# A hybrid decoder block with 64 experts on one core: other load sizes and room order in the expert pass, paired products in the gate pieces, idle products before the last transposes

## The chip, the cores and the metric

The kernel runs on one core of one Trainium2 chip. The metric is device time in microseconds (us) of one launch. Before the change, three runs took 1255.89, 1257.45 and 1258.70 us (median 1257.45). One more execution was profiled; it took 1255.22 us.

## The reference

All tensors are float32. 16 meta tokens are put ahead of 256 tokens of width 1024, so 272 rows go through the block.

```
hn   = rms_norm(h, norm_mix)
u, z, xbc, dt, g_pool, g_ssd = split(hn @ w_in)          # w_in: 1024 x 8224
y_pool = pool_mixer(u) @ w_pool_out                      # causal window means of 2, 4, 8, 16 rows
y_ssd  = ssd_mixer(z, xbc, dt) @ w_ssd_out               # Mamba-2 scan, 32 heads, chunks of 128
h = h + (sigmoid(g_pool) * y_pool + sigmoid(g_ssd) * y_ssd) @ w_out
x2 = rms_norm(h, norm_ffn)
# one expert group of 8 per token, then 2 of its 8 experts
y = sum over the token's 2 experts e: weight * (silu(x2 @ w_gate[e]) * (x2 @ w_up[e])) @ w_down[e]
out = rms_norm(h + y, norm_final)[16:]
```

The 64 experts' weights are 403 MB: w_gate_up is 64 x 1024 x 1024 and w_down 64 x 512 x 1024. All of them are read, whatever the routing.

## The kernel before

**Front.** `w_in` and the smaller weights come as 98 pieces of 128 x 1024, two to a load of 1 MB ("chunk", `load_w`, L194), into a ring of four chunks. The order of the work is written by hand: step n computes piece n (`proj`, L448, for the first 64) and then runs what was put down for that step (`at(n, ...)`, `hooks`). Float32 products are made of three products of split operands: `mm3` multiplies high by high, high by low and low by high. `split_piece` (L270) makes the high and the low half of a piece three pieces ahead: ScalarE (ACT) copies the high half, VectorE (DVE) or, for some pieces, GpSimd (POOL) subtracts it to get the low one. The second half of a chunk, once split, triggers the load of the chunk four further on. The 16 gate pieces ("gp" and "gs", steps 48 to 63) each end in one ACT Sigmoid read from PSUM. Then come the pooling products ("pw", L705 to L708), whose activations `pool_s(w)` splits on DVE into tiles "ah" and "al" of a pool of six buffers each (`asplit_f`); the splits for w = 0 to 2 are put down for steps 56, 58 and 60, the one for w = 3 stands inside the pooling stage, behind its first products. After them come "po" (8 pieces), "so" (16) and "wo" (8), then the router.

**Experts.** Experts are taken four at a time: 16 quads. A quad's weights are 24 rooms of 1 MB (128 partitions x 2048 floats): 16 of gate/up, read in `up(q, xT)`, and 8 of down, read in `down(q)`. Room m is number m mod 24 of quad m // 24. `load_e` (L207) issues the loads on SyncE's queue (SP), in order. The first 24 rooms are single loads into 24 places that come free one by one while the front still runs (arena, "aux", "ws", "mg"). From room 24 on, loads are of two rooms (2 MB, 16 KB per partition), into 11 places: eight in the arena, issued as the first pass gives them up (`freed`, L184: after rooms 1, 4, 6, 7, 9, 13, 16, 19), and three "pair" tiles, issued after room 23. From there on every odd room, once used (`used`, L227), issues the next load into the place it leaves. The last eight rooms are single loads again. At most eight loads are under way: each waits for the landing of the one eight before.

**One quad on TensorE (PE).** `up`: 128 matmuls of 32 x 512 per operand half, four per room; then two transposes (L958), the gather of the next quad's tokens (L933), `glu` (ACT Silu, DVE product, four transposes at L952, ACT copy), `down`: two halves of four rooms, each followed by an ACT copy and `combine` (L971), which adds into four PSUM accumulators. In the last quad `keep_warm` puts idle products (ones by ones) between rooms of `down` (`WARM`, L23: three each behind rooms (0,2), (0,3), (1,0), (1,1), (1,2), as half and room).

## Time and profile before

| what | value |
|---|---|
| runs, median | 1257.45 us (1255.89 to 1258.70) |
| the profiled execution | 1255.22 us, its span 1253.5 us |
| PE busy | 959.0 us, 77% of the span |
| DVE, ACT, POOL busy | 319.4, 291.2, 141.5 us |
| moved | 462.06 MB, mean 369 GB/s |

The span is what the page and all rows count from; the 1.7 us around it are launch and end. Engines overlap, so busy shares do not add up to the span: what matters is which wait ends last at each place. PE holds two sorts of row: PE for matmuls, PEld for loading the stationary operand, which runs beside them. A matmul's duration includes the time in which it overlaps its neighbours, so the pace of a run of matmuls is read from the distance of their starts. In rows of a time line the number in square brackets is the engine's idle time before the row, and what ended it.

### The profile page before, as it was taken

To read this page: it belongs to the slowest core of one execution; us is meant where nothing else is said; L and a number is where in the kernel's file an instruction comes from. 1 tells how busy PE (TensorE), PEld (TensorE's weight loads), DVE (VectorE), ACT (ScalarE), POOL (GpSimd) and SP (SyncE) were. 2 spreads that over 40 slices of the span, in tenths; PEclk is the share of its full clock that TensorE was granted. 3 is DMA by queue.
4 is the path that set the end of the run, shared out by engine and by line. 5 is a ranking of instruction groups with operands and counts; after the bars stand their busy time and mean duration, and the time that the engine had idled before them with its cause. 6 is when DMAs were issued, how large, how long until landed. Compare 5 with 4: busy or idle time off the path is not lost.

```text
span 1253.5 us, 15661 instructions
## 1 busy us (share of the span) xinstructions
PE 959.0 (77%) x6721; PEld 538.0 (43%) x6721; DVE 319.4 (25%) x529; ACT 291.2 (23%) x558; POOL 141.5 (11%) x118
## 2 busy tenths in 40 slices
PE   9999999999997767576775757575658666666766
PEld 9999999999853321212221212131222212121312
DVE  6899986668731000000000000000000000000001
ACT  7887756433331100101010101010100101010102
POOL 2334444334100000000000000000000000000000
PEclk9999999999999898888888888888988797888788
DMA  7544447667899999999999999999999999999996
GB/s 290 185 157 165 168 140 268 266 216 258 344 407 430 430 430 432 430 431 430 431 430 431 429 431 429 431 430 431 430 431 429 432 430 432 429 431 430 432 427 264
DMA packets 39656, 462.06 MB, mean 369 GB/s; under 512 B 4424, under 2 KB 4752, under 8 KB 6816
## 3 DMA queue, kind: packets, MB, share of 16 engines
q1 hardware_dynamic: 39216, 459.95, 88.3%
q8 instruction: 54, 0.88, 0.3%
q10 hardware_dynamic: 368, 1.08, 0.2%
q14 instruction: 18, 0.15, 0.0%
HBM read 459.93 MB, written 1.08 MB: 368 GB/s over the span
## 4 chain that ended last, share of the span: by engine, by line
DMA 62%; PE 26%; DVE 7%; ACT 3%; issue 1%; SPq 0%; POOL 0%; DVEq 0%; ACTq 0%; POOLq 0%
DMA arena<-gu 28%; DMA pair<-gu 15%; DMA arena<-dn 12%; DMA pair<-dn 6%; PE pj L297 3%; PE pj L299 3%; PE pj L298 3%; DVE whl L280 3%; PE pg L1045 1%; PE pg L1056 1%; PE pu L1045 1%; PE pj L769 1%; PE gx L933 1%; DVE arena L462 1%; PE so L298 1%
## 5 line engine op out<-in xcount | busy, mean ns | idle before, releaser
L1045 PE MATMUL pg<-arena,xT 128*32 128x512 f32 x776 | 121.8, 703 | 125.4 <-DMA arena<-gu 125.4
L959 DVE COPY aux<-tr 128x256 f32<-128x256 f32 x16 | 6.8, 425 | 682.6 <-PE tr L958 682.6
L924 ACT ACTIVATE xT<-gx,csta 128x128 f32<-128x128 f32 x124 | 35.4, 368 | 530.5 <-PE gx L933 522.8
L297 PE MATMUL pj<-hnh,whl 128*128 128x256 f32 (+1 forms) x512 | 149.7, 292 | 0.0
L299 PE MATMUL pj<-hnh,whl 128*128 128x256 f32 (+1 forms) x512 | 145.9, 285 | 0.4 <-DVE whl L280 0.4
L298 PE MATMUL pj<-hnl,whl 128*128 128x256 f32 (+1 forms) x512 | 145.7, 285 | 0.1
L1045 PE MATMUL pu<-arena,xT 128*32 128x512 f32 x768 | 125.1, 729 | 0.0
L280 DVE TENSOR_TENSOR whl<-arena,whl 128x1024 fp32r<-128x1024 f32 x79 | 115.2, 1465 | 30.4 <-ACT whl L279 29.9
L1045 PEld LDWEIGHTS pg<-arena,xT 128*32 128x32 f32 x776 | 18.6, 114 | 220.6 <-DMA arena<-gu 185.2
L975 POOL TENSOR_TENSOR aux<-sel,wte 128x128 f32<-128x128 f32 x32 | 12.2, 401 | 829.9 <-DVE sel L876 786.4
L279 ACT ACTIVATE whl<-arena 128x1024 fp32r<-128x1024 f32 x86 | 90.5, 1056 | 54.2 <-PE so L299 29.5
L297 PEld LDWEIGHTS pj<-hnh,whl 128*128 128x128 f32 x512 | 96.5, 189 | 2.5 <-issue 2.0
L298 PEld LDWEIGHTS pj<-hnl,whl 128*128 128x128 f32 x512 | 96.4, 188 | 1.2 <-issue 1.2
L299 PEld LDWEIGHTS pj<-hnh,whl 128*128 128x128 f32 x512 | 96.5, 189 | 0.6 <-DVE whl L280 0.6
L933 PE MATMUL gx<-sel,xh 128*128 128x128 f32 x480 | 65.0, 291 | 29.3 <-ACT xT L924 18.6
L971 PE MATMUL acc<-aux 128*128 128x512 f32 x128 | 63.5, 618 | 24.0 <-ACT aux L969 23.2
L1045 PE MATMUL pg<-pair,xT 128*32 128x512 f32 x240 | 41.4, 769 | 50.7 <-DMA pair<-gu 50.6
L933 PEld LDWEIGHTS gx<-sel,xh 128*128 128x128 f32 x480 | 59.1, 201 | 36.9 <-ACT xT L924 21.7
L1045 PEld LDWEIGHTS pu<-arena,xT 128*32 128x32 f32 x768 | 28.7, 127 | 72.5 <-issue 72.5
L1056 PE MATMUL pg<-arena,aux 128*32 128x512 f32 x328 | 53.9, 806 | 6.9 <-ACT aux L953 6.9
L280 POOL TENSOR_TENSOR whl<-arena,whl 128x1024 fp32r<-128x1024 f32 x19 | 47.8, 2521 | 74.1 <-ACT whl L279 73.7
L971 PEld LDWEIGHTS acc<-aux 128*128 128x128 f32 x128 | 21.7, 189 | 67.9 <-ACT aux L969 50.8
(343 smaller groups left out, 1208.6 us busy)
## 6 DMA issues: line engine op xcount, KB each, us to landing
arena<-gu SPq DMA_DIRECT2D x90, 2048.0 KB, 38.9
arena<-dn SPq DMA_DIRECT2D x38, 2048.0 KB, 38.9
pair<-gu SPq DMA_DIRECT2D x30, 2048.0 KB, 38.9
arena<-wf SPq DMA_DIRECT2D x48, 1024.0 KB, 4.9
pair<-dn SPq DMA_DIRECT2D x18, 2048.0 KB, 38.8
arena<-gu SPq DMA_DIRECT2D x13, 1024.0 KB, 8.1
arena<-dn SPq DMA_DIRECT2D x11, 1024.0 KB, 25.6
arena<-rows_d SPq DMA_DIRECT2D x8, 512.0 KB, 5.7
```

Source lines behind the costliest of these rows:

```text
L279: S.activation(wh, w, AF.Copy)
L280: (G if n in on_pool else V).tensor_tensor(out=wl, in0=w, in1=wh.bitcast(FT), op=OP.subtract)
L297: T.matmul(ps, wh, ah, start=start, stop=False, skip_group_check=True)
L298: T.matmul(ps, wh, al, start=False, stop=False, skip_group_check=True)
L299: T.matmul(ps, wl, ah, start=False, stop=stop, skip_group_check=True)
L462: V.scalar_tensor_tensor(out=acc[:, j:], in0=ps[:, :NA - j], scalar=cs("cw", ct * 4 + 3 - j), in1=acc[:, j:], op0=OP.mult, op1=OP.add)
L769: T.matmul(wo[2 * t + h], lw, rw[:, h * 512:(h + 1) * 512], start=kk == 0 and f, stop=kk == 7 and l, skip_group_check=True)
L924: S.activation(xT[:, 4 * b + k, :], ps[:, k * 128:(k + 1) * 128], AF.Copy, scale=cs("nf", 4 * b + k))
L933: T.matmul(ps[:, k * 128:(k + 1) * 128], xh[:, t, (4 * b + k) * 128:(4 * b + k + 1) * 128], sel[:, t, :], start=t == 0, stop=t == 1, skip_ ...
L971: T.matmul(acc[t][h], ctv[:, t * 128:(t + 1) * 128], yv, start=first, stop=last, skip_group_check=True)
L1045: T.matmul(ps[32 * e:32 * e + 32], xT[:, k, 32 * e:32 * e + 32], w[:, e * 512:(e + 1) * 512], start=k == 0, stop=k == 7, skip_group_check= ...
L1056: T.matmul(py[32 * e:32 * e + 32], hsT[:, c, 32 * e:32 * e + 32], w[:, e * 512:(e + 1) * 512], start=c == 0, stop=c == 3, skip_group_check ...
```

## The change

It does seven things.

- **Gate pieces.** `hnh` and `hnl` become one tile `hn`, with high and low side by side. `mm2` multiplies a gate piece's high half by both in one product of 512 columns, then its low half by the high activations. The two sums lie in two halves of the bank; `halves` copies one on ACT and adds the other on DVE, and one Sigmoid of 128 x 1024 follows every fourth piece.
- **Split buffers.** The pool of "ah" and "al" has eight buffers each, and `pool_s(3)` is put down for step 62.
- **First pass.** There are 25 rooms: a new tile "extra" takes room 24 at step 40. One place of the chunk ring is given to room 8 at step 81: chunk 41 triggers no load, so each of the last four chunks is issued two steps later, and rooms 13 to 16 change places.
- **Second pass.** Rooms 25 to 39 are loaded by nine loads: three single ones and six pairs, issued after rooms 0, 1, 4, 6, 7, 8, 10, 14 and 19.
- **4 MB loads.** From room 40 on, loads are of four rooms (4 MB, 32 KB per partition) into five places: a tile "four", issued after room 23, and four arena places, issued after rooms 33, 35, 37 and 39; then after every fourth room. There are 84 of them. The weights are laid out for it in memory. The last eight rooms stay single.
- **Last quad.** 12 idle products stand behind room 11 of `up`, five in front of the four transposes, two behind them; those in `down` are 2, 2, 3, 3 instead of five times 3.
- Small tiles move to other places ("tri", "sum2", "small", "st", "stri").

```
-WARM = {(0, 2): 3, (0, 3): 3, (1, 0): 3, (1, 1): 3, (1, 2): 3}
+WARM = {(0, 3): 2, (1, 0): 2, (1, 1): 3, (1, 2): 3}
...
+    extra = keep.tile([128, 2048], FT, name="extra")
...
+    slots = [s_xs[0], s_xs[1], s_rw[1], s_bt[0], s_bt[1], s_bt[3], s_rw[0], s_bt[2], r_w[0], s_yn[0], s_yn[1]]
     ONCE = len(slots)
...
+    slots += [None, None, r_w[2], r_w[3], r_w[1], "mgA", r_ws[0], s_ce[0], s_ce[1], r_ws[1], "mgB", r_ws[2], r_ws[3], extra]
...
+    again = {0: (25, 1, s_xs[0]), 1: (26, 1, s_xs[1]), 4: (28, 2, two(a_bt)), 6: (30, 2, two(a_row)), 7: (32, 2, two(a_bt + 2 * SLOT)),
+             8: (27, 1, r_w[0]), 10: (34, 2, two(a_yn)), 14: (36, 2, two(a_w + 2 * SLOT)), 19: (38, 2, two(a_ce))}
...
+    rooms = [None] + [ar[:, i * 4 * SLOT:(i + 1) * 4 * SLOT] for i in (3, 2, 0, 1)]
+    frees = [23, 33, 35, 37, 39] + list(range(NS2 + 3, 16 * 24, 4))
...
+    SK = NCHUNK - 8
+
+    def w_slot(i):
+        return wview[(i + 3) % NW if i < SK + 4 else 1 if i == SK + 7 else i % NW]
...
+    def load_4():
+        m = n_4[0]
+        n_4[0] += 4
         if m >= 16 * PER:
             return
...
         if m < 16 * PER - 8:
-            nc.sync.dma_start(out=rooms[(m - NS) // 2 % NP], in_=src)
+            nc.sync.dma_start(out=rooms[(m - NS2) // 4 % 5], in_=src_of(m, 4))
         else:
...
-        if m == NS - 1:
+        if m == 23:
             right.close()
...
+            rooms[0] = p.tile([128, 4 * SLOT], FT, name="four")
+        if m in again:
+            a_, n_, r_ = again[m]
+            nc.sync.dma_start(out=r_, in_=src_of(a_, n_))
+        if m in frees:
+            load_4()
...
-    asp = aspctx.enter_context(tc.tile_pool(name="asp", bufs=6))
+    asp = aspctx.enter_context(tc.tile_pool(name="asp", bufs=8))
...
-        if h == 1:
+        if h == 1 and ch != SK:
             load_w()
...
+    def mm2(ps, wh, wl, a, start, stop):
+
+        T.matmul(ps.rearrange("p (i n) -> p i n", n=NT), wh, a, start=start, stop=False, skip_group_check=True)
+        T.matmul(ps[:, 0:NT], wl, a[:, 0, :], start=False, stop=stop, skip_group_check=True)
+
+    def halves(out, ps):
+
+        S.activation(out, ps[:, NT:2 * NT], AF.Copy)
+        V.tensor_tensor(out=out, in0=out, in1=ps[:, 0:NT], op=OP.add)
...
-            S.activation((sgp if kind == "gp" else sgs)[:, i, :], ps[:, :NT], AF.Sigmoid)
+            v = sgp if kind == "gp" else sgs
+            halves(v[:, i, :], ps)
+            if i % 4 == 3:
+                steps.setdefault(n + 1, []).insert(0, (sigmoid, (v[:, i - 3:i + 1, :],)))
...
-        if w < 3:
-            at(56 + 2 * w, pool_s, w)
-    for n_ in (46, 46, 46, 57, 58, 68, 74, 80, 82, 89):
+        at(56 + 2 * w, pool_s, w)
+    at(40, load_1, NS - 1)
+    for n_ in (46, 46, 46, 57, 58, 68, 74, 80, 81, 82, 88):
         at(n_, load_e)
...
-        if w == 1:
-            pool_s(3)
...
+        if warm:
+            keep_warm("gx", 5)
         ps = bank(mps, "tr", 1)
...
+                if q == 15 and (k, h) == (5, 1):
+                    keep_warm("gx", 12)
```

In the order on DVE, before, the two pairs of splits of `pool_s(3)` (L305 and L306) stand inside the pooling stage, between its evacuations from PSUM (L708); L280 is the low half of a weight piece:

```order
L280 TENSOR_TENSOR whl<-arena,whl 128x1024 x2
L708 SCALAR_TENSOR_TENSOR poA<-pj,csta,poA 128x256 x2
L305 CAST ah<-arena 128x256
L306 TENSOR_TENSOR al<-arena,ah 128x256
L305 CAST ah<-arena 128x256
L306 TENSOR_TENSOR al<-arena,ah 128x256
L708 SCALAR_TENSOR_TENSOR poA<-pj,csta,poA 128x256
```

Of the change, the same stretch; L334 is the addition in `halves`, L340 and L341 are the splits, L748 the evacuation:

```order
L305 TENSOR_TENSOR whl<-arena,whl 128x1024
L334 TENSOR_TENSOR arena<-arena,pj 128x256
L340 CAST ah<-arena 128x256
L341 TENSOR_TENSOR al<-arena,ah 128x256
L340 CAST ah<-arena 128x256
L341 TENSOR_TENSOR al<-arena,ah 128x256
L334 TENSOR_TENSOR arena<-arena,pj 128x256
L748 SCALAR_TENSOR_TENSOR poA<-pj,csta,poA 128x256 x3
```

The two pairs of splits now stand ahead of the last gate piece's addition, so no split is left between the evacuations.

On SP, the last single load of the first pass ("room") and what follows it, before:

```order
L218 DMA room<-dn 128x2048
L222 DMA arena<-gu 128x4096 x8
L222 DMA pair_4127<-dn 128x4096
L222 DMA pair_4129<-dn 128x4096
L222 DMA pair_4131<-dn 128x4096
```

And of the change:

```order
L234 DMA room<-dn 128x2048
L261 DMA arena<-gu 128x2048 x2
L261 DMA arena<-gu 128x4096 x3
L261 DMA arena<-gu 128x2048
L261 DMA arena<-gu 128x4096 x3
L248 DMA four<-dn 128x8192
L248 DMA arena<-dn 128x8192
```

Up to the use of room 23 the old order has issued 11 loads of 2 MB, the new one 15 MB in nine loads and one of 4 MB; the next load is then issued after room 25 in the old order, after room 33 in the new.

On PE, the last quad from its last `up` rooms to its first `down` rooms, of the change (L936 is the idle product, L1094 `up`, L1007 and L999 the transposes, L1107 `down`):

```order
L936 MATMUL gx<-ones 128x128 x12
L1094 MATMUL pg<-arena,xT 32x512 x4
L1094 MATMUL pu<-arena,xT 32x512 x4
L1094 MATMUL pg<-arena,xT 32x512 x4
L1094 MATMUL pu<-arena,xT 32x512 x4
L1007 MATMUL tr<-ident,aux 128x128 x2
L936 MATMUL gx<-ones 128x128 x5
L999 MATMUL tr<-ident,aux 128x128 x4
L936 MATMUL gx<-ones 128x128 x2
L1107 MATMUL pg<-arena,aux 32x512 x16
L936 MATMUL gx<-ones 128x128 x2
```

Before, the three rows with 12, 5 and 2 idle products are not there; the first idle products stand behind the third room of `down`.

## Rows read from the trace of the kernel before

**Rows 1.** The page's chain that ended last, by engine.

```profile
DMA 62%; PE 26%; DVE 7%; ACT 3%; issue 1%; SPq 0%; POOL 0%; DVEq 0%; ACTq 0%; POOLq 0%
```

**Rows 2.** Windows: stretch, us, busy by engine (count), PEclk, DMA share, GB/s.

```profile
245.00:250.00 5.00, 2.85 (x17) 2.45 (x16) 4.93 (x9) 1.88 (x4) 2.65 (x2) 0.88 0.60 210
250.00:255.00 5.00, 5.00 (x36) 5.00 (x35) 3.00 (x6) 2.20 (x3) 0.00 (x0) 0.78 0.18 28
...
340.00:355.00 15.00, 15.00 (x113) 13.84 (x113) 9.40 (x40) 3.64 (x8) 0.00 (x0) 1.00 1.01 424
355.00:365.00 10.00, 10.00 (x94) 3.91 (x96) 2.52 (x12) 5.40 (x19) 0.00 (x0) 1.00 0.95 367
...
460.00:1220.00 760.00, 507.00 (x3166) 166.09 (x3162) 22.54 (x65) 61.83 (x158) 9.87 (x26) 0.85 1.01 430
```

**Rows 3.** Time line of ACT, gate pieces: start, us, engine, line, operation.

```profile
207.29 0.39 ACT L473 ACTIVATE arena<-pj 128x256 f32<-128x256 f32 x1 [0.85 <-PE pj L299]
...
210.13 0.39 ACT L473 ACTIVATE arena<-pj 128x256 f32<-128x256 f32 x1 [1.51 <-PE pj L299]
```

**Rows 4.** Time line of PE, products of 512 columns in the "wo" pieces.

```profile
341.65 0.39 PE L769 MATMUL pj<-whl,mgB 128*128 128x512 f32 x1
...
342.33 0.39 PE L769 MATMUL wo<-whl,mgB 128*128 128x512 f32 x1
```

**Rows 5.** Time line of PE in the pooling stage.

```profile
246.19 0.28 PE L297 MATMUL so<-ah,whl 128*128 128x256 f32 x1
248.55 0.41 PE L298 MATMUL so<-al,whl 128*128 128x256 f32 x1 [2.08 <-DVE al L306]
```

**Rows 6.** Time lines of POOL and DVE in the same stretch.

```profile
245.75 2.46 POOL L280 TENSOR_TENSOR whl<-arena,whl 128x1024 fp32r<-128x1024 f32 x1 [0.56 <-ACT whl L279]
...
246.04 2.46 DVE L306 TENSOR_TENSOR al<-arena,ah 128x256 fp32r<-128x256 f32 x1
```

**Rows 7.** Time line of DVE, beside the gate pieces and in the "po" pieces.

```profile
210.59 1.74 DVE L603 RECIPROCAL arena<-arena 128x256 f32<-128x256 f32 x1
212.36 2.71 DVE L605 SCALAR_TENSOR_TENSOR arena<-arena,csta 128x256 f32<-128x256 f32 x4
...
222.65 0.76 DVE L621 SCALAR_TENSOR_TENSOR arena<-arena 128x256 f32<-128x256 f32 x2 [3.50 <-POOL arena L617]
...
259.15 0.41 DVE L722 TENSOR_TENSOR arena<-arena,pj 128x256 f32<-128x256 f32 x1
```

**Rows 8.** Time line of ACT, an activation of 128 x 1024.

```profile
200.47 1.15 ACT L600 ACTIVATE arena<-arena,epst 128x1024 f32<-128x1024 f32 x1
```

**Rows 9.** The page's DMA issues: engine, count, KB each, median us to landing.

```profile
arena<-gu SPq DMA_DIRECT2D x90, 2048.0 KB, 38.9
...
arena<-wf SPq DMA_DIRECT2D x48, 1024.0 KB, 4.9
```

**Rows 10.** Time line of SP, the load that room 25 issues.

```profile
401.44 0.33 SPq L222 DMA_DIRECT2D arena<-dn  x1
```

**Rows 11.** Time line of PE, quads 1 and 2: rooms 25, 33 and 58.

```profile
400.34 1.04 PE L1045 MATMUL pu<-arena,xT 128*32 128x512 f32 x8
...
407.20 1.04 PE L1045 MATMUL pu<-arena,xT 128*32 128x512 f32 x8
...
449.97 1.07 PE L1045 MATMUL pg<-arena,xT 128*32 128x512 f32 x8 [1.79 <-DMA arena<-gu]
```

**Rows 12.** Time line of all engines, the last quad.

```profile
1222.94 1.07 PE L1045 MATMUL pg<-pair,xT 128*32 128x512 f32 x8 [1.49 <-DMA pair<-gu]
...
1227.82 4.48 PE L1056 MATMUL pg<-arena,aux 128*32 128x512 f32 x24 [0.69 <-ACT aux L953]
...
1232.22 0.94 PE L891 MATMUL gx<-ones 128*128 128x128 f32 x6
...
1234.93 1.98 PE L971 MATMUL acc<-aux 128*128 128x512 f32 x4
...
1242.47 0.16 PEld L1056 LDWEIGHTS pu<-arena,aux 128*32 128x32 f32 x8 [0.16 <-DMA arena<-dn]
```

More of the change, by code (lines that the diff above doesn't have):

```diff
@@ L165, in block @@
-    NS = len(slots)
-    rooms = [ar[:, o:o + 2 * SLOT] for o in (a_xs, a_bt, a_row, a_bt + 2 * SLOT, a_yn, a_w, a_w + 2 * SLOT, a_ce)]
-    freed = [1, 4, 6, 7, 9, 13, 16, 19]
-    NP = len(freed) + 3
-    def slot(m):
-        if m < NS:
-            return slots[m]
-        return half_of(rooms[(m - NS) // 2 % NP], m % 2)
-    def half_of(v, h):
-        return v[:, h * SLOT:(h + 1) * SLOT]
+    assert a_row == 4 * SLOT and a_yn == 8 * SLOT and a_bt == 12 * SLOT
+    r_w = [ar[:, a_w + i * SLOT:a_w + (i + 1) * SLOT] for i in range(4)]
@@ new lines, in block @@
+    NS = len(slots)
+    assert NS == 25
+    two = lambda o: ar[:, o:o + 2 * SLOT]
+    again = {0: (25, 1, s_xs[0]), 1: (26, 1, s_xs[1]), 4: (28, 2, two(a_bt)), 6: (30, 2, two(a_row)), 7: (32, 2, two(a_bt + 2 * SLOT)),
+             8: (27, 1, r_w[0]), 10: (34, 2, two(a_yn)), 14: (36, 2, two(a_w + 2 * SLOT)), 19: (38, 2, two(a_ce))}
+    NS2 = NS + sum(n for _, n, _ in again.values())
+    assert NS2 == 40
+    slots += [None] * (NS2 - NS)
+    for m_, n_, r_ in again.values():
+        for j_ in range(n_):
+            slots[m_ + j_] = r_[:, j_ * SLOT:(j_ + 1) * SLOT]
@@ L200, in load_w @@
             else:
[L201 removed]
+                nc.sync.dma_start(out=w_slot(i), in_=wf[i])
             n_w[0] += 1
@@ L760, in block @@
             merge(k + 2)
-        for _ in range((3, 1, 0, 1, 0, 1, 0, 0)[k]):
+        for _ in range((3, 0, 1, 0, 0, 0, 0, 0)[k]):
             load_e()
@@ L770, in block @@
                              skip_group_check=True)
-        for _ in range((0, 0, 0, 1, 1, 3, 0, 0)[k]):
+        if k == 3:
+            load_1(16)
+        for _ in range((0, 0, 0, 0, 2, 3, 0, 0)[k]):
             load_e()
+            if n_e[0] == 16:
+                n_e[0] += 1
     def half(v, h):
@@ L792, in block @@
         load_e()
-    last = wsp.tile([128, SLOT], FT, name="room", tag=slots[-1], bufs=1)
-    slots[-1] = last
+    last = wsp.tile([128, SLOT], FT, name="room", tag=slots[NS - 2], bufs=1)
+    slots[NS - 2] = last
     it = mt([128, 64 + 8 + 128], "it")
```

104 lines of the change are left out of this document (53 added, 51 removed).

## The prediction

> **What bounds the kernel now.** I read four views, in this order. The chain of waits gives DMA 62% of the span [rows 1]. The windows show where: from 460 to 1220 us the queue moves 430 GB/s without a gap, while PE is busy 507 of 760 us [rows 2]. So the second half is a stream of expert weights at a fixed rate, and its end is its start, plus the bytes that are left, plus holes, plus what PE has to do behind the last room. The time lines of PE, DVE and ACT then show the front, in which PE sets the pace: a gate piece starts every 2.84 us, and ACT waits for PE each time [rows 3]. The time line of the last quad shows that the last room is waited for by only 0.16 us [rows 12]: PE is just ready when it lands. A gain therefore has three places: the front gets shorter (all later events move with it), the stream starts with more rooms or runs faster, or the tail gets shorter.
>
> In what follows, times are those of the profiled execution (1255.22 us, span 1253.5); its clock is kept, and the shift of the front is added at the end. The three timed runs lie 0.7 to 3.5 us above it, their median 2.2.
>
> **Gate pieces.** A piece is 24 products of 256 columns in 2.84 us, 0.118 each [rows 3]. Products of 512 columns start every 0.227 us (three steps in 0.68) [rows 4]. A piece becomes 8 x (0.227 + 0.118) = 2.76 us, so 16 pieces give back 16 x 0.08 = 1.3 us. On ACT a copy takes the place of the Sigmoid, with the same size, and a Sigmoid of 128 x 1024 comes on every fourth piece, 1.15 us by the nearest row [rows 8]; ACT waits 1.51 us per piece now [rows 3], which covers it. On DVE there is one addition of 0.41 us per piece [rows 7]. That is the doubtful part: it must wait for PE's piece, and what stands behind it in order waits too. Behind piece 52 stand the reciprocal and four products of 1.74 + 2.71 us [rows 7], and behind those the low half of piece 56. Now DVE has 3.50 us to spare by 222.65 [rows 7], when the stretch of pool sums ends; the seven additions up to there take 2.9 of it. I count a delay of PE of 0.6 us there, between 0 (DVE just keeps up) and 1.5 (it is late by half of a piece), and 0.2 us in the pooling stage, where ACT now has one Sigmoid more ahead of its evacuations.
>
> **Split buffers.** In the pooling stage PE starts a product at 246.19 and the next at 248.55 [rows 5]; at its pace of 0.12 that is a hole of 2.24 us. It ends with a DVE split that took 2.46 us while POOL's 2.46 us subtraction was running [rows 6]. After the hole the granted clock falls: 0.88 and 0.78 in two windows of 5 us [rows 2], so (0.12 + 0.22) x 5 = 1.7 us of PE time are lost at the lower of the two levels, 1.2 GHz. With eight buffers the splits of w = 3 stand at step 62, in front of the last gate piece's end, so neither the hole nor the slow stretch should be there: -3.9 us. What is late next there is the evacuation of the last pooling product, by at most the 0.2 us above. The front is then shorter by 1.3 + 3.9 - 0.6 - 0.2 = 4.4 us, with ends at 2.5 (the additions cost 1.5 and a shorter hole stays) and 5.2 (no new delay).
>
> The ring's four last chunks come two steps (5.7 us) later. A chunk takes 4.9 us to land [rows 9], and each is wanted about five steps after its new issue, 14 us, so this costs nothing; the cover is gone if more than three or four single loads are queued ahead of it.
>
> **Room 24 and the opening.** I count in rooms that have landed. Before, PE waits at 449.97 for room 58, which comes with room 59 in one load [rows 11], so 60 rooms have landed then. Going back 36 rooms at 38.9 / 16 = 2.43 us each [rows 9], and the opening's loss of 10 x (1 - 367/430) = 1.5 us between 355 and 365 [rows 2], 24 rooms had landed by 361. Of the change, 25 rooms land by the same time, since the additional one goes into a part of the front where the queue idles. The nine loads of 15 MB follow from there without the 1.5 us, because the first goes out one room earlier: 361 + 15 x 2.43 = 397.4. The 4 MB of "four", issued after room 23, join them and land at 407.1. The next load waits until room 33 is used. Its matmuls start at 407.20, 0.86 per room [rows 11], so it is used at 408.1; the issue follows 0.2 us behind (room 25: used at 401.2, issued at 401.44 [rows 10, 11]), and the way from issue to landing costs 4.9 - 2.4 = 2.5 us beyond the bytes [rows 9]. Four loads of 4 MB then bring rooms 44 to 59, and 60 rooms have landed at 408.3 + 2.5 + 16 x 2.42 = 449.5. So the 25th room (2.4 us) and the closed opening (1.5) are eaten by a new hole of some 3.5 us at about 406, in which the queue is empty: -0.5 us instead of -3.9. The hole's far end hangs on PE alone, so a small delay ahead of it changes nothing. Bounds: +1.5, if PE is slower through quad 1, and -2, if it is faster.
>
> **4 MB loads.** No row shows one. The nearest pair: 2 MB loads land every 38.9 / 8 = 4.86 us, 2.431 per MB [rows 9]; the last eight single loads take (1242.47 - 1222.94) / 8 = 2.441 [rows 12]. Half as many load ends are worth 0.010 us per MB, so the next halving 0.005 x 336 MB (84 loads) = 1.7 us. By the windows single loads run at 424 and 2 MB loads at 430 GB/s [rows 2]: 1.4%, the half of it on 336 MB (816 us at 432 GB/s) is 5.7 us. The other end is nothing, or a loss (the slower side below). I take -1.7, since landings are what PE waits for.
>
> The Trainium skill (DMA: Bandwidth & Descriptors, Bandwidth) has a rule that larger loads are faster, with 341 GB/s at 1 MB and 425 at 16 MB for loads issued from GpSimd. By it 4 MB loads would be worth tens of us. The trace does not agree: with eight under way, 1 MB loads already land at 2.44 us, and the sum goes by these rows.
>
> Five places of 4 MB hold 20 MB, 11 of 2 MB held 22. A place comes back late at the turn from `up` to `down`: in the last quad 12 us lie between the last rooms of `up` and the first combine [rows 12], and the other quads have a gather in between as well. Behind a place that is given back stand at least three full loads, 29 us, so the stream should not run dry there.
>
> **Last quad.** The last four rooms of `up` now land together, when the last two do now, at 1222.94. Four rooms take 4 x 0.86 = 3.4 us instead of 1.7. Down starts now 4.88 us after the landing, so at 1222.94 + 4.88 + 1.7 = 1229.5. The seven products around the transposes lie in gaps that exist. Three idle products take 0.94 us [rows 12]. Four rooms 3.4, two idle products beside the ACT copy 0.6, combine 1.98, three rooms 2.6, eight idle products 2.5: PE is ready at 1240.6, 1.9 us before the last room at 1242.47. This holds at full clock; one slow stretch like that of [rows 2] costs 1.7 and uses it up. The 12 products behind room 11 take 3.8 us, or 7.5 at the lower clock, in a wait of 9.7 between two loads less 3.4 to 7 for four rooms: at worst they end some 4 us late. I take +0.3, from 0 to +2.5.
>
> **Sum.** -4.4 - 0.5 - 1.7 + 0.3 = -6.3, so 1255.2 becomes 1248.9 in the profile's terms and 1251.1 against the median. I forecast 1250.8.
>
> **Rivals.**
> - *The additions hold PE in the gate pieces.* DVE becomes the bound from step 52 to 62, and each piece takes what DVE needs. For: 2.9 of 3.5 us of slack go. Against: the halves are made three pieces ahead of PE. At 3.0 us a piece instead of 2.76 the 16 pieces take 3.8 us more, and of the front's 4.4 us 0.6 are left: -2.5 in all, 1255.0.
> - *The larger loads give the windows' 1.4%.* -5.7 instead of -1.7: 1246.8.
> - *The stream runs dry at each turn of a quad*, because one place is a fifth of the buffer. For: the first hole is of this kind. Against: 29 us of queue for a lag of 12 and a gather. If 13 turns each lost 0.5 us, the time would be 1257.3; it decides from 0.5 us a turn.
> - *Longer rows come slower (the slower side).* Rows of 32 KB per partition stand twice as far apart in memory. If 336 MB came at the 424 GB/s of the single loads instead of 430 [rows 2], 352 million bytes would take 831 us instead of 819, +12: 1264.5. It turns the gain into a loss from a rate of 427 down. Against: going from 8 to 16 KB gained. The Trainium skill (DMA: Bandwidth & Descriptors, Latency and other measured facts) tells of such a loss for row pitches at large powers of two, from 512 KiB up; no run here shows one.
>
> **How the numbers follow.** Forecast 0.68, additions 0.12, windows' rate 0.08, dry turns 0.06, longer rows 0.06. The forecast's own range is 1246.5 to 1254.5; with the windows' rate and the additions, 1245.5 to 1256.5 holds eight of ten. About 0.2% (2.5 us) is what a measurement of this kernel can tell from no change. Faster: forecast, windows' rate and a third of the additions, 0.80; same: the rest of the additions and dry turns with small prices, 0.12; slower: longer rows and deep dry turns, 0.08.
>
> **What would show it.** PE without a gap over 0.5 us and at full clock from 240 to 255; gate pieces 2.76 us apart; the matmuls of room 25, at 400.34 now [rows 11], 4 to 5 us earlier; a window of under 300 GB/s some 5 us behind that, and no other until the end; 4 MB landings every 9.7 us (9.9 would be the slower side); the last room waited for. It is wrong if gate pieces stay at 2.84 or more, if a second hole shows in the stream, or if PE is not waiting for the last room.

## The result, and the profile after

| | median, us | lowest to highest | ratio to before, 95% interval |
|---|---|---|---|
| before (measured beside it) | 1255.91 | 1255.36 to 1258.70 | |
| changed kernel | 1249.45 | 1249.34 to 1250.29 | 0.9948 [0.9937, 0.9960] |

The forecast was 1250.8, the likeliest case. The profiled execution took 1250.28 us with a span of 1248.7; that of before 1255.22 and 1253.5, so the two traces differ by 4.9 us, the medians by 6.5.

The chain of waits of the changed kernel, by engine, where [rows 1] had DMA at 62% (the chain is one path among nearly equal ones, so the share says less than the sum below):

```profile
DMA 43%; PE 40%; DVE 9%; ACT 6%; issue 2%; POOL 0%; ACTq 0%; DVEq 0%; SPq 0%; POOLq 0%
```

Its windows (stretch, us, busy by engine with counts, granted clock, DMA share, GB/s), beside [rows 2]:

```profile
245.00:250.00 5.00, 5.00 (x45) 5.00 (x44) 3.87 (x9) 4.32 (x10) 4.27 (x2) 1.00 0.42 134
250.00:255.00 5.00, 5.00 (x44) 5.00 (x43) 4.96 (x8) 2.00 (x2) 2.41 (x1) 1.00 0.85 311
...
350.00:355.00 5.00, 5.00 (x50) 2.48 (x53) 0.00 (x0) 4.24 (x14) 0.00 (x0) 1.00 0.87 295
...
370.00:380.00 10.00, 4.93 (x32) 3.42 (x36) 1.43 (x6) 4.36 (x10) 0.61 (x3) 0.74 1.02 436
395.00:400.00 5.00, 5.00 (x35) 1.43 (x38) 1.50 (x9) 0.00 (x0) 0.00 (x0) 0.66 0.98 419
400.00:405.00 5.00, 5.00 (x52) 1.53 (x48) 0.00 (x0) 0.00 (x0) 0.00 (x0) 1.00 0.33 134
405.00:410.00 5.00, 5.00 (x52) 1.56 (x48) 0.00 (x0) 0.00 (x0) 0.00 (x0) 1.00 0.71 256
...
460.00:1220.00 760.00, 522.64 (x3210) 179.21 (x3206) 22.52 (x65) 61.73 (x158) 9.87 (x26) 0.83 1.00 432
```

Three things are to be seen. The pooling stage (245 to 255 us) is full and at full clock, where PE was busy 2.85 of 5 us. The stream has the hole that was forecast, at 400 to 410 us: 134 and 256 GB/s, where 430 would be full. That is (296 + 174) x 5 = 2.35 MB, or 5.5 us of the queue by bytes; between landings, as the forecast counted its 3.5 us, it is 3.1 (the last section has both). And from 460 us on it runs at 432, not 430. The clock is down at 370 to 380 and at 395 to 400, which matters below.

The gate pieces on ACT (start, us, engine, line, operation), as [rows 3]:

```profile
206.96 0.39 ACT L333 ACTIVATE arena<-pj 128x256 f32<-128x256 f32 x1 [1.47 <-PE pj L329]
...
209.76 0.39 ACT L333 ACTIVATE arena<-pj 128x256 f32<-128x256 f32 x1 [1.47 <-PE pj L329]
```

They are 2.80 us apart: forecast 2.76, before 2.84. DVE at the place where 3.50 us were to spare [rows 7]:

```profile
222.66 0.76 DVE L663 SCALAR_TENSOR_TENSOR arena<-arena 128x256 f32<-128x256 f32 x2 [2.01 <-POOL arena L659]
```

It still has 2.01 us: up to here the additions cost 1.5 us of the slack, where 2.9 were counted, and hold up nobody. A smaller hole than that of [rows 5] is left on PE, and at another place: at the first pooling product of w = 1. The products take three PSUM banks ("pj") in turn, and this one needs the bank that the last gate piece's addition (L334) reads:

```profile
241.62 0.28 PE L324 MATMUL pj<-ah,whl 128*128 128x256 f32 x1
242.39 0.39 PE L322 MATMUL pj<-ah,whl 128*128 128x256 f32 x1 [0.50 <-DVE arena L334]
```

and on DVE and POOL at the same time, as in [rows 6]:

```profile
239.50 2.51 DVE L341 TENSOR_TENSOR al<-arena,ah 128x256 fp32r<-128x256 f32 x1
241.93 0.41 DVE L334 TENSOR_TENSOR arena<-arena,pj 128x256 f32<-128x256 f32 x1
```

```profile
239.17 2.56 POOL L305 TENSOR_TENSOR whl<-arena,whl 128x1024 fp32r<-128x1024 f32 x1 [16.54 <-ACT whl L304]
```

So the split of 2.51 us beside POOL's subtraction is still there (the one before it takes 0.42); but now it only delays the addition behind it, and by that PE waits 0.5 us.

**Where the time went, from trace to trace** (after less before; landings are those that the trace gives for the loads' issues):

| milestone | before | after | difference | added on the way |
|---|---|---|---|---|
| first matmul of room 0 | 356.40 | 351.48 | -4.9 | -4.9 |
| 60 rooms landed | 449.93 | 448.07 | -1.9 | +3.0 |
| last load of the last `up` landed | 1222.90 | 1217.38 | -5.5 | -3.7 |
| end of the span | 1253.5 | 1248.7 | -4.8 | +0.7 |

### The profile page after: what moved, and what is told of

Its sections match the earlier page's. It is cut to its first block, busy times and chain, and to the rows that moved or that the text cites. A ratio compares the mean times of both kernels' runs of the same rounds, so it can differ in the third digit from the quotient of the medians.

```text
span 1248.7 us, 15306 instructions
## 1 busy us (share of the span) xinstructions
PE 969.6 (78%) x6621; PEld 542.6 (43%) x6621; DVE 322.8 (26%) x545; ACT 293.2 (23%) x561; POOL 142.6 (11%) x118
## 4 chain that ended last, share of the span: by engine, by line
DMA 43%; PE 40%; DVE 9%; ACT 6%; issue 2%; POOL 0%; ACTq 0%; DVEq 0%; SPq 0%; POOLq 0%
DMA arena<-gu 32%; PE pg L1107 7%; DMA four<-gu 5%; PE gx L978 5%; PE pg L1094 4%; PE pu L1094 4%; DMA arena<-dn 3%; DVE whl L305 3%; ACT xT L969 3%; PE pj L328 2%; PE pj L322 2%; PE pj L324 2%; PE pj L323 2%; DMA four<-dn 2%; DVE arena L498 1%
## 5 line engine op out<-in xcount | busy, mean ns | idle before, releaser
L1094 PE MATMUL pg<-arena,xT 128*32 128x512 f32 x816 | 145.0, 791 | 123.0 <-DMA arena<-gu 123.0
L1094 PE MATMUL pu<-arena,xT 128*32 128x512 f32 x824 | 134.7, 732 | 0.0
L305 DVE TENSOR_TENSOR whl<-arena,whl 128x1024 fp32r<-128x1024 f32 x79 | 115.3, 1462 | 26.4 <-ACT whl L304 25.8
L1094 PEld LDWEIGHTS pg<-arena,xT 128*32 128x32 f32 x816 | 27.1, 134 | 213.5 <-DMA arena<-gu 144.8
L322 PE MATMUL pj<-hn,whl 128*128 128x272 f32 (+1 forms) x384 | 113.6, 296 | 0.0
L324 PE MATMUL pj<-hn,whl 128*128 128x272 f32 (+1 forms) x384 | 109.7, 286 | 0.4 <-DVE whl L305 0.4
L323 PE MATMUL pj<-hn,whl 128*128 128x272 f32 (+1 forms) x384 | 109.5, 285 | 0.1
L978 PE MATMUL gx<-sel,xh 128*128 128x128 f32 x480 | 61.5, 281 | 29.2 <-ACT xT L969 18.6
L1107 PE MATMUL pg<-arena,aux 128*32 128x512 f32 x400 | 69.2, 852 | 9.6 <-ACT aux L1002 7.1
L322 PEld LDWEIGHTS pj<-hn,whl 128*128 128x128 f32 x384 | 72.4, 188 | 2.5 <-issue 1.5
L323 PEld LDWEIGHTS pj<-hn,whl 128*128 128x128 f32 x384 | 72.6, 189 | 1.2 <-issue 1.2
L1094 PEld LDWEIGHTS pu<-arena,xT 128*32 128x32 f32 x824 | 32.7, 137 | 92.5 <-issue 92.5
L324 PEld LDWEIGHTS pj<-hn,whl 128*128 128x128 f32 x384 | 72.3, 188 | 0.6 <-DVE whl L305 0.6
L978 PEld LDWEIGHTS gx<-sel,xh 128*128 128x128 f32 x480 | 55.8, 192 | 36.2 <-ACT xT L969 21.4
L1094 PE MATMUL pg<-four,xT 128*32 128x512 f32 x192 | 37.2, 859 | 38.6 <-DMA four<-gu 38.6
L305 POOL TENSOR_TENSOR whl<-arena,whl 128x1024 fp32r<-128x1024 f32 x19 | 48.5, 2555 | 69.0 <-ACT whl L304 69.0
```

The source lines that it names most:

```text
L305: (G if n in on_pool else V).tensor_tensor(out=wl, in0=w, in1=wh.bitcast(FT), op=OP.subtract)
L322: T.matmul(ps, wh, ah, start=start, stop=False, skip_group_check=True)
L323: T.matmul(ps, wh, al, start=False, stop=False, skip_group_check=True)
L324: T.matmul(ps, wl, ah, start=False, stop=stop, skip_group_check=True)
L978: T.matmul(ps[:, k * 128:(k + 1) * 128], xh[:, t, (4 * b + k) * 128:(4 * b + k + 1) * 128], sel[:, t, :], start=t == 0, stop=t == 1, skip_ ...
L1094: T.matmul(ps[32 * e:32 * e + 32], xT[:, k, 32 * e:32 * e + 32], w[:, e * 512:(e + 1) * 512], start=k == 0, stop=k == 7, skip_group_check= ...
```

## Experiments

Twelve kernels were run, each an edit of the changed kernel, four at a time with before beside them (medians of before 1255.88, 1255.93 and 1254.83). The changed kernel itself has 1249.45. The ratio and its interval are worked out from all executions, so the ratio need not be the quotient of the medians. Before is about 1 us lower beside the last four (no_25th, early_pairs, pairs_61, warm_q0) than beside the others; by ratios, what these four gain on the changed kernel is about 1 us less than by medians.

| run | median, us | lowest to highest | ratio to before, 95% |
|---|---|---|---|
| gates_three | 1250.27 | 1247.31 to 1250.61 | 0.9945 [0.9927, 0.9963] |
| split_late | 1255.15 | 1252.59 to 1258.49 | 0.9994 [0.9982, 1.0007] |
| two_mb | 1250.59 | 1250.49 to 1251.30 | 0.9952 [0.9935, 0.9969] |
| no_idle | 1250.39 | 1247.54 to 1251.76 | 0.9948 [0.9930, 0.9967] |
| early_half | 1245.90 | 1244.91 to 1250.36 | 0.9922 [0.9903, 0.9940] |
| rows_16k | 1254.02 | 1250.92 to 1257.34 | 0.9987 [0.9975, 0.9999] |
| last_four | 1253.04 | 1250.91 to 1254.14 | 0.9975 [0.9966, 0.9984] |
| all_three | 1248.77 | 1248.04 to 1250.53 | 0.9944 [0.9929, 0.9960] |
| no_25th | 1249.37 | 1247.63 to 1254.28 | 0.9957 [0.9939, 0.9975] |
| early_pairs | 1246.08 | 1245.65 to 1247.03 | 0.9927 [0.9909, 0.9945] |
| pairs_61 | 1244.61 | 1243.96 to 1247.71 | 0.9918 [0.9899, 0.9936] |
| warm_q0 | 1245.88 | 1244.08 to 1250.93 | 0.9927 [0.9905, 0.9948] |

There is one trace per kernel, and executions of one kernel differ by 1 to 7 us, so a trace can stand away from its median; where it does, the text says so.

### The front: gates_three and split_late

```
-            if wide or kind == "z":
+            if True:
                 mm3(ps[:, :w], wh[:, k * 128:(k + 1) * 128], wl[:, k * 128:(k + 1) * 128],
...
-            halves(v[:, i, :], ps)
-            if i % 4 == 3:
-                steps.setdefault(n + 1, []).insert(0, (sigmoid, (v[:, i - 3:i + 1, :],)))
+            S.activation(v[:, i, :], ps[:, :NT], AF.Sigmoid)
```

> The changed kernel with the gate pieces as before: 24 products of 256 columns and one Sigmoid per piece, no addition on DVE. Theory: the trace after shows pieces 2.80 us apart, 2.84 before, so the front gets 16 x 0.04 = 0.6 us longer and the time 0.6 us more (within 0.2% of the changed kernel). The prediction's own term was 1.3 - 0.6 = 0.7 by another way (2.76 us a piece and a delay of DVE): the sums are nearly the same, the spacing in the trace tells them apart (2.84 here, and DVE's slack at piece 56 back from 2.0 to about 3.5 us). Rival: the additions cost DVE as much as PE gains elsewhere, and the time is the same or 0.5 us less.

```
-        at(56 + 2 * w, pool_s, w)
+        if w < 3:
+            at(56 + 2 * w, pool_s, w)
...
 for w in range(4):
+        if w == 1:
+            pool_s(3)
         if w % 2 == 0:
             hooks(n)
```

> The changed kernel with the splits of pool_s(3) back inside the pooling stage (eight buffers kept). Theory: the hole of some 2.2 us and the slow stretch behind it (1.7 us) come back at 247 us, room 0 starts 3.5 to 4 us later, and so do the hole's far end at 406 us and the end: +3.9 us. Rival: of a shift of the front only 2 to 2.5 us reach the stream, as the trace after shows (4.9 us earlier at room 0, 2.5 at room 33), since PE is at the lower clock in parts of quads 0 and 1 whenever it waits there: +2.0 to +2.5. Second rival: the stretch does not come back with the hole; +2.2.

gates_three: 1250.27, 0.8 us more, with intervals that overlap almost wholly. Its evacuations are again 2.84 apart (207.18 and 210.02), and DVE's slack is back at 3.51; but the gap of 0.5 us at 242 is gone, and the first "wo" product starts at 317.15, after 317.18. So the gates' part is worth nothing that can be told: 16 x 0.04 us less PE time, given back by the gap.

split_late: 1255.15, all but the whole gain lost. PE in its pooling stage:

```profile
246.25 0.38 PE L322 MATMUL so<-ah,whl 128*128 128x256 f32 x1 [1.48 <-DVE ah L340]
248.75 0.51 PE L323 MATMUL so<-al,whl 128*128 128x256 f32 x1 [2.12 <-DVE al L341]
```

Both waits end with a split, and the clock behind them is 0.77 in the window from 250 to 255 us. "wo" starts at 322.17 and room 0 at 356.46, 5.0 us later, as in before (322.04 and 356.40). In the twelve other traces with the earlier splits "wo" starts between 315.05 and 318.19, so this shift is not chance. The theory's 3.5 to 4 was somewhat low for the front. Of the 5.0 us its trace shows 2.8 at 60 rooms landed (450.90) and 2.3 at the end, as the rival said. What is missing is lost by the load behind room 33: it goes out at 408.36, 2.6 us after that of the changed kernel (405.79). Between room 0 and that load PE ran at 1.2 GHz for 3.41 us here, and for 10.24 us in the changed kernel's trace (table under warm_q0). But the traced execution was the fastest of twelve, and the median is 5.7 us above the changed kernel's. So the rival holds for this pair of traces, and which of the two holds for most executions stays open; that this part carries most of the gain is shown.

### The rate of the stream: two_mb and rows_16k

```
-            nc.sync.dma_start(out=rooms[(m - NS2) // 4 % 5], in_=src_of(m, 4))
+            for j in (0, 2):
+                nc.sync.dma_start(out=rooms[(m - NS2) // 4 % 5][:, j * SLOT:(j + 2) * SLOT], in_=src_of(m + j, 2))
```

> The changed kernel with each 4 MB load of the second pass as two of 2 MB into the two halves of the same place (rows in memory unchanged, 16 KB of each per load). Theory: a load's end costs queue time, 0.044 us for each of some 84 more, so the stream takes 3.7 us longer, as between 60 rooms landed and the last whole load of the two traces (769.3 us after, 773.0 before): +3.7 us. The prediction's size: +1.7. Rival: the rate comes from the rows' order in memory, or from fewer and larger places, not from the loads' size: 0 to +0.5.

```
-        v = gu_d[q, i // 4] if i < 16 else dn_d[q, (i - 16) // 4]
-        return v[:, (m % 4) * SLOT:(m % 4 + n) * SLOT]
+        v, i = (gu_d, i) if i < 16 else (dn_d, i - 16)
+        if n == 4:
+            return v[q, i // 2:i // 2 + 2].rearrange("b p n -> p b n")
+        return v[q, i // 2][:, (i % 2) * SLOT:(i % 2 + n) * SLOT]
...
-            nc.sync.dma_start(out=rooms[(m - NS2) // 4 % 5], in_=src_of(m, 4))
+            nc.sync.dma_start(out=rooms[(m - NS2) // 4 % 5].rearrange("p (b n) -> p b n", b=2), in_=src_of(m, 4))
...
-    gu = f["w_gate_up"][0].reshape(16, 4, 4, 2, 128, 2, 512).transpose(0, 2, 4, 3, 5, 1, 6).reshape(16, 4, 128, 8192)
+    gu = f["w_gate_up"][0].reshape(16, 4, 8, 128, 2, 512).transpose(0, 2, 3, 4, 1, 5).reshape(16, 8, 128, 4096)
...
```

> The changed kernel with the expert weights in memory as before (16 KB per partition of one block, two blocks per 4 MB load), so that each 4 MB load reads two rows of 16 KB per partition instead of one of 32 KB; number and size of the loads unchanged. Theory A: the gain of the 4 MB loads is one per load (0.040 us for each of 84 that go away; the two-halves experiment took 772.6 us for the stretch that takes 769.3 after): 0 here. Theory B: it is one per row (packet), and the halves lost it because their rows were cut to 16 KB too: +3.3 us, 4 MB landings about 9.71 apart instead of 9.67.

The stretch is read from PE's waits, early and at the last `up`. After:

```profile
448.12 1.93 PE L1094 MATMUL pg<-arena,xT 128*32 128x512 f32 x8 [6.03 <-DMA arena<-gu]
...
1217.42 1.07 PE L1094 MATMUL pg<-arena,xT 128*32 128x512 f32 x8 [1.52 <-DMA arena<-gu]
```

rows_16k:

```profile
445.86 1.93 PE L1096 MATMUL pg<-arena,xT 128*32 128x512 f32 x8 [6.04 <-DMA arena<-gu]
...
1218.09 1.07 PE L1096 MATMUL pg<-arena,xT 128*32 128x512 f32 x8 [0.74 <-DMA arena<-gu]
```

two_mb, where the first of the two waits is for room 61, not 59:

```profile
451.14 1.87 PE L1095 MATMUL pg<-four,xT 128*32 128x512 f32 x8 [2.88 <-DMA four<-gu]
...
1218.90 1.06 PE L1095 MATMUL pg<-arena,xT 128*32 128x512 f32 x8 [1.50 <-DMA arena<-gu]
```

Per room of 1 MB: after 769.30 / 316 = 2.4345 us; rows_16k 772.23 / 316 = 2.4438; two_mb 767.76 / 314 = 2.4451; before, from [rows 11, 12], 772.97 / 316 = 2.4461. The packet counts of the pages go with it: rows_16k has 10752 more than after, that is 84 loads of 128 rows, one packet per row. After, rows_16k, two_mb:

```profile
DMA packets 27847, 462.04 MB, mean 370 GB/s; under 512 B 3112, under 2 KB 3440, under 8 KB 5504
```

```profile
DMA packets 38599, 462.04 MB, mean 370 GB/s; under 512 B 3112, under 2 KB 3440, under 8 KB 5504
```

```profile
DMA packets 39944, 462.05 MB, mean 370 GB/s; under 512 B 4456, under 2 KB 4784, under 8 KB 6848
```

rows_16k has the same loads of 4 MB as after, and the rate of two_mb. So it is the length of a row in memory (32 KB against 16 KB) that gives 2.9 of the 3.7 us, and not the number of loads (0.4): theory B. My theory A, and the reasoning of the prediction, which went by load ends, fall. The ten other traces with 32 KB rows agree: 769.1 to 770.1 us between the same two landings.

two_mb's 1250.59 is only 1.1 above the changed kernel, since its halves also went out earlier (the first when room 29 was used): 60 rooms had landed at 446.21. rows_16k's median lies 4.6 above, 1.7 more than this stretch explains; its trace is of its fastest execution, and where the others lost more is not shown.

### The tail: no_idle and last_four

```
-                if q == 15 and (k, h) == (5, 1):
-                    keep_warm("gx", 12)
...
-        glu(pg, pu, rs, q == 15)
+        glu(pg, pu, rs)
```

> The changed kernel without the 12 idle products behind room 11 of the last quad and the 5 + 2 around its transposes (WARM as in the changed kernel). Theory: PE then runs parts of the last quad at the lower clock; in the trace after it waits 1.18 us for the last room, which covers one short stretch and no more: 0 to +1.5 us, with the last room no longer waited for. Rival 1: the wait covers all: 0 (within 0.5 us). Rival 2: two or more slow stretches fall into `down`: +2.5 to +4 us.

```
-        if m < 16 * PER - 8:
+        if m < 16 * PER - 4:
             nc.sync.dma_start(out=rooms[(m - NS2) // 4 % 5], in_=src_of(m, 4))
```

> The changed kernel with rooms 376 to 379 as one 4 MB load, only the last four rooms as single loads. Theory: the last single load goes out late in the trace after (issued at 1217.44, landing 2.92 us behind the one before it instead of 2.45), since eight loads are under way and one more waits for a landing; with three loads fewer it is issued earlier, and three load ends fewer are paid: -0.5 to -0.6 us, the four rooms landing together at about 1227.0 and PE through them and the combine by 1232.5, before room 381 is needed. Rival: PE gets late by the four rooms that come at once: +0.5 to +2.

The changed kernel's last quad, beside [rows 12]:

```profile
1224.02 2.78 PE L1107 MATMUL pg<-arena,aux 128*32 128x512 f32 x24 [0.24 <-ACT aux L1002]
1227.15 1.06 PE L1107 MATMUL pg<-arena,aux 128*32 128x512 f32 x8 [0.35 <-DMA arena<-dn]
...
1237.54 1.07 PE L1107 MATMUL pu<-four,aux 128*32 128x512 f32 x8 [0.99 <-DMA four<-dn]
```

no_idle is 0.9 above by medians, with overlapping intervals, and its trace ends 0.3 earlier. Its last room landed at 1236.91 and was begun 0.3 us later:

```profile
1237.21 1.06 PE L1105 MATMUL pu<-four,aux 128*32 128x512 f32 x8
```

From the last landing to the end it takes 11.4 us, the changed kernel 11.2: rival 1, the wait covers all but 0.2 us of them.

last_four went the other way. Its stream did gain: 19.6 us from the last `up` to the last landing instead of 20.1, as the theory said. But PE is late:

```profile
1224.12 6.34 PE L1107 MATMUL pg<-arena,aux 128*32 128x512 f32 x32 [3.43 <-DMA arena<-dn]
...
1238.50 1.06 PE L1107 MATMUL pu<-four,aux 128*32 128x512 f32 x8
```

PE waits 3.43 us for the four rooms that land together, and then takes 6.34 us for them at the lower clock (0.50 from 1222.8 to 1229.6) instead of 3.4. The last room, landed at 1233.92, begins at 1238.50. The four rooms' arrival one by one kept PE fed; that is worth more than the 0.5 us of the queue. The rival was right in kind, at 15.4 instead of 11.2 us behind the last landing; by medians last_four is 3.6 us above the changed kernel, more than the 2 at which it ended.

### The hole: early_half, no_25th, early_pairs, warm_q0

```
-        if m in frees:
-            load_4()
+        if m in (29, 33):
+            j = 0 if m == 29 else 2
+            nc.sync.dma_start(out=rooms[1][:, j * SLOT:(j + 2) * SLOT], in_=src_of(44 + j, 2))
+            if m == 33:
+                n_4[0] += 4
+        elif m in frees:
+            load_4()
```

> The changed kernel with the first load into the places of rooms 28, 29, 32 and 33 cut in two: its first half is issued when room 29 is used, its second half when room 33 is. Theory: the queue is empty for some 3 us behind the landing of 'four' (405.17 us in the trace after, next landing 417.91, 9.67 of it transfer), since one load waits for PE to use room 33; with the first half out by 402.4 it lands at about 410.0, the second at 414.9, and all behind it 3.0 us earlier: 60 rooms at 445.1 instead of 448.07, the time 3.0 us less. Rival: the hole costs nothing, since PE or the places given back later hold the stream anyway: 0. Second rival: only part of it, since the half lands 4.4 us after its issue at the earliest and the queue is empty up to there: -1.5 to -2.

1245.90: 3.5 us less, with intervals that overlap by 0.0003. In its trace 60 rooms had landed at 445.57, 2.5 earlier, with PE no earlier than in the changed kernel. The hole is on the path, and the rival (0) is out.

```
-    at(40, load_1, NS - 1)
...
+        if m == 0:
+            load_1(NS - 1)
         if m in again:
```

> The changed kernel with room 24 loaded at the head of the second round (when room 0 is used) and no longer at step 40 of the front, so that 24 rooms, not 25, are loaded ahead; the order of all other loads is kept. Theory (the hole eats the 25th room): everything up to 'four' lands 2.4 us later, 'four' at 407.6 instead of 405.2, the hole behind it is 0.6 us instead of 3.1, and the load that waits for room 33 lands as before at about 417.9: 0, at most +0.5. Rival: the room is worth its transfer: +2.4. Second rival: with nearly no hole left, PE waits for rooms in quad 1, and it is more than +2.4.

1249.37, no difference (1.1 us more by ratio, with intervals that overlap): the 25th room alone is worth nothing, as the prediction had it. But not quite by the way that I wrote. Its windows:

```profile
350.00:355.00 5.00, 5.00 (x51) 1.89 (x53) 0.00 (x0) 4.91 (x18) 0.00 (x0) 1.00 1.02 421
...
400.00:405.00 5.00, 5.00 (x52) 1.56 (x48) 0.00 (x0) 0.00 (x0) 0.00 (x0) 1.00 0.09 36
405.00:410.00 5.00, 5.00 (x46) 1.37 (x38) 0.00 (x0) 0.00 (x0) 0.00 (x0) 1.00 0.97 367
```

In the changed kernel the queue waits 1.6 us at 350 to 355 (295 GB/s) for room 0's place; here the additional load fills that wait, so "four" came at 402.88 and not at 407.6, and the hole stays at 5.3 us. With the room the queue loses 1.6 us at that wait, and what is left of its 2.4 falls into the hole.

```
+    pairs = {26: (44, two(a_xs)), 27: (46, two(a_w)), 29: (48, two(a_bt)), 31: (50, two(a_row)), 33: (52, two(a_bt + 2 * SLOT)),
+             35: (54, two(a_yn)), 37: (56, two(a_w + 2 * SLOT)), 39: (58, two(a_ce))}
...
-    frees = [23, 33, 35, 37, 39] + list(range(NS2 + 3, 16 * 24, 4))
+    frees = [23, 43, 53, 55, 57, 59] + list(range(63, 16 * 24, 4))
...
-        n_4[0] += 4
+        n_4[0] += 4 if m > NS2 else 20
...
+        if m in pairs:
+            nc.sync.dma_start(out=pairs[m][1], in_=src_of(pairs[m][0], 2))
```

> The changed kernel with rooms 44 to 59 loaded as eight pairs into places that come free one by one (behind rooms 26, 27, 29, 31, 33, 35, 37, 39), not as four loads of 4 MB behind rooms 33, 35, 37, 39. Theory: with the early half the queue was still empty for 2.4 us (its half went out at 403.12 and landed at 410.94, behind a last landing of about 403.6); the first pair now goes out at about 399, so no hole is left, 60 rooms have landed at some 443 us instead of 448.07 (16 rooms at 2.43 behind 'four', where the hole began), and the time is 5 us less than the changed kernel's: 1244.5, 1.5 to 2.4 under the early half. Rival: the hole's rest is in front of PE's use of rooms anyway (PE or places given back late hold the stream behind room 60): as the early half, 1246. Second rival: a new hole opens at rooms 64 to 79, whose places now come back 1.5 rooms later per load: slower than the early half.

1246.08: 3.4 us less than the changed kernel (2.6 by ratio; the intervals overlap), not the 5 expected, and no better than the early half by medians. Its trace shows the step as expected, 60 rooms at 443.39 (4.7 earlier) and the end 4.6 earlier, and no new hole behind; only 1.3 us of hole are left in one window:

```profile
400.00:405.00 5.00, 5.00 (x52) 1.52 (x48) 0.00 (x0) 0.00 (x0) 0.00 (x0) 1.00 0.85 318
```

```
-            keep_warm("gx", 5)
+            keep_warm("gx", warm)
...
-        glu(pg, pu, rs, q == 15)
+        glu(pg, pu, rs, {0: 12, 15: 5}.get(q, 0))
```

> The changed kernel with 12 idle products in front of the transposes of quad 0 and 2 behind them (as the last quad has 5 and 2), in a wait of 3.67 us. Theory: in the trace after PE runs at 1.2 GHz from 374.85 to 381.68 us, through six rooms of quad 0; with the wait filled that stretch goes, PE uses room 33 1.7 to 3.4 us earlier, the hole's far end comes by as much, up to the hole's 3.1 us: -1.7 to -3.0 us. Rival: the clock falls there all the same, or some microseconds later, since the other small waits stay: 0, or +0.3 for the products. It would also tell whether the executions that differ by 2 to 4 us differ by this stretch.

1245.88: 3.6 us less (2.6 by ratio), with intervals that overlap. PE in quad 0 and the windows of it, with the issue of the load that waits for room 33:

```profile
373.30 2.94 PE L936 MATMUL gx<-ones 128*128 128x128 f32 x24 [0.89 <-ACT xT L969]
```

```profile
370.00:380.00 10.00, 8.85 (x76) 6.78 (x80) 1.44 (x6) 3.71 (x7) 0.62 (x3) 1.00 1.01 431
...
395.00:400.00 5.00, 5.00 (x52) 1.53 (x48) 0.00 (x0) 0.00 (x0) 0.00 (x0) 1.00 0.99 423
```

```profile
401.43 0.33 SPq L248 DMA_DIRECT2D arena<-dn  x1
```

The same issue in the changed kernel:

```profile
390.07 0.33 SPq L248 DMA_DIRECT2D four<-dn  x1
405.79 0.33 SPq L248 DMA_DIRECT2D arena<-dn  x1
```

The clock is 1.00 where it was 0.74 and 0.66; the load goes out 4.4 us earlier, of which 0.7 come from the front of that execution (room 0 at 350.79). 60 rooms had landed at 443.83. So PE's clock in quads 0 and 1 sets the hole's far end, and fourteen idle products move the landing of 60 rooms by some 3.5 us.

The other traces agree. This is the time from room 0's first matmul to the issue of the load that waits for room 33 (of its second half, where the load is cut), by how long PE ran at 1.2 GHz on the way:

| at 1.2 GHz, us | room 0 to the issue, us | traces |
|---|---|---|
| 0 | 50.6 | warm_q0 |
| 3.41 | 51.9 to 52.0 | before, split_late, last_four, rows_16k |
| 6.83 | 53.6 and 54.0 | no_idle, no_25th |
| 10.24 | 54.3 to 54.7 | the changed kernel, gates_three, two_mb, early_half, all_three |

The changed kernel's 10.24 us are 6.83 from 374.85 on and 3.41 from 395.33 on; rows_16k and last_four have neither the second stretch nor half of the first, and 60 rooms had landed 2.3 and 2.9 us earlier. Before the first of them PE had been busy 2.39 of 5 us (370 to 375). no_idle and last_four are the changed kernel up to the last quad and its loads, so the stretches differ between executions of one program. What decides them is not shown.

### Together: all_three and pairs_61

```
-        at(56 + 2 * w, pool_s, w)
+        at(56 + 2 * w - (w == 3), pool_s, w)
```

all_three has this edit, that of early_half and that of last_four; pairs_61 has it with the edit of early_pairs.

> The changed kernel with the early half, the last four single loads only, and pool_s(3) one step earlier (step 61), so that its splits do not meet a subtraction on POOL (the trace after still shows one split of 2.51 us at 239.5 and a gap of 0.5 us on PE at 242.4). Theory: -3.0 - 0.5 - 0.4 = -3.9 us, 1245.5. Rival: the front's 0.4 us is swallowed by PE's lower clock in quads 0 and 1 and the early half is worth only 1.5: -2.0, 1247.4. Second rival: the split at step 61 meets the window sums on POOL instead and costs PE a gap: no better than the early half alone.

> The same eight pairs and pool_s(3) one step earlier (step 61). Theory: the gap of 0.5 us on PE at 242 goes, and the front is 0.4 us shorter: 0.4 us under the eight pairs alone. Rival: other waits between the front and room 0 take it back (in the run with three changes wo began 1.4 us earlier and room 0 only 0.2 to 0.9): 0.

all_three, 1248.77, misses its 1245.5 by last_four's tail: 14.8 us from the last landing to the end. Its stream was the earliest but one (60 rooms at 442.97). pairs_61 is the fastest kernel here, 1244.61, 4.8 us below the changed one (3.8 by ratio); its interval ends at 0.9936, just under where that of the changed kernel begins. In neither trace is there a gap on PE over 0.4 us at 235 to 262. That the step earlier alone gives the 1.5 us between pairs_61 and early_pairs is not shown: "wo" starts 1.1 us earlier, about what that start differs by between kernels with the same front. warm_q0 and pairs_61 were not run together.

## Why the prediction was right, step by step

- **Split buffers, -3.9: right, somewhat low.** Hole and slow stretch went as described; split_late puts them at 5.0 us at room 0, and at 5.7 by medians.
- **Gate pieces, -1.3, and the additions on DVE, +0.6, pooling stage +0.2: near zero in sum, as measured, but by other sizes.** A piece gave back 0.04 us, not 0.08. The additions delayed no piece; their price was the 0.5 us at 242, when one of them stood behind a split of 2.51 us; gates_three has neither additions nor gap, and "wo" starts at the same time. The front in all: -4.9, forecast -4.4. The rival of the additions is out, since DVE kept 2.01 us.
- **Opening and 25th room, -0.5: the term that was off. It measured +3.0, outside its own bounds (-2 to +1.5).** The hole was forecast at the right place, with PE deciding its far end, and "if PE is slower through quad 1" was named.
  - The step that failed is taking the 407.20 of the old trace and moving it by the front's shift alone: the load went out at 405.79, not at 408.3 - 4.4 = 403.9, although the front gave 4.9. PE took 54.3 us from room 0 to that issue, 2.4 more than before, with 10.24 us of it at 1.2 GHz where before has 3.41; warm_q0 shows that this stretch at the lower clock sets the issue. That the front's shift caused it is not shown: last_four and rows_16k have the earlier front too, and 3.41 us.
  - Another 1.1 us is the second load behind the hole, which took 10.82 us instead of 9.67. It takes 10.8 to 11.1 in all eight traces where a whole 4 MB load is the first behind the hole, and 9.7 in early_half, where a half is; so it is no accident of one execution, and its cause is open.
  - The near end came about as forecast: the opening's loss, counted as closed, stood at 350 to 355 (1.6 us), but 25 rooms had landed at 355.71, 0.9 us ahead of 361 - 4.4, and "four" ended between 401.5 and 404.8, forecast 402.7.
- **4 MB loads, -1.7: right in sign, half the size, wrong in cause.** -3.7, by the length of the rows. The Trainium skill (DMA: Bandwidth & Descriptors, Why small descriptors are slow (HBM only)) names two fixed costs: about 3 cycles per packet on a bus with beats of 32 bytes, and 32 bytes of metadata per descriptor. By them half as many rows would be worth 3/512 - 3/1024 = 0.29% and 32/16384 - 32/32768 = 0.10%, together 0.39% or 3.0 us of 769, an estimate that takes each row as one packet and one descriptor; the traces agree, with 0.38% or 2.9 us (rows_16k against the changed kernel). That these costs are the cause is not shown by that.
- **Tail, +0.3: +0.7.** PE was covered, by a wait of 0.99 us for the last room where 1.9 were worked out. The 0.4 us beyond it are the last single load, which landed 2.92 us behind the one before.

-4.9 + 3.0 - 3.7 + 0.7 is -4.8 in the spans (before rounding); the forecast sum was -6.3. The medians' -6.5 lie nearer to it than the traces, since the profiled execution of the changed kernel was 0.8 us above its median and that of before 0.7 below its own. Two errors of opposite sign, +3.5 for the hole and -2.0 for the larger loads, met in the sum; that the time came nearer than its parts is luck.

Of the signs named ahead, a window under 300 GB/s at the hole and none from 410 to 1215 us, landings every 9.7 us, full clock in the pooling stage and the wait for the last room came. Two did not quite: gate pieces are 2.80 us apart, midway between the 2.76 of the forecast and the 2.84 of a failure, and the matmuls of room 25 start at 397.15, 3.2 us earlier and not 4 to 5.

The rivals: dry turns of quads did not occur (4 MB landings mostly 9.65 to 9.72 us apart, with single ones of 10 to 10.8 now and then, as before has of 5.8 to 6.0 among its 4.85). Longer rows were not slower. The windows' rate (1.4%) was too much; the rate rose by 0.5%. The ring's later chunks, counted at nothing, show no price: up to 340 us no wait of PE over 0.2 us ends with a load, before or after.

## What to carry over

When a load waits for a consumer to give back its place, look at which consumer step sets it: here a few idle products in one wait, or a load cut in two so that its first half goes out earlier, were each worth about 3 us (2.6 to 3.6), with intervals that touch or overlap that of the changed kernel; the front's repair was worth 5.7. Here the stream's rate went by the length of the contiguous rows (2.9 us of 769) and hardly by the size of the loads (0.4), so merging loads without merging the rows would have gained next to nothing. Before moving the last loads together, count what PE loses at the lower clock while it waits for the larger one.
